# New cost figures and a shared port in the planner that orders a hybrid encoder's instructions

## The chip, the core and the metric

The kernel runs on one core of one Trainium2 chip. A core has five engines, each with an instruction queue of its own that runs in order: TensorE (PE), VectorE (DVE), ScalarE (ACT), GpSimd (POOL) and SyncE (SP), which here issues the DMA transfers. An instruction waits on semaphores for what other engines must have done. The metric is the device time of one execution in microseconds (us).

## What is computed

Two sequences (prompt and sample) of 1024 rows of 1024 channels go through the same two layers and a final norm. Cut to what matters:

```python
def mixer_layer(x, ...):
    hdn = rmsnorm(x, norm_g)
    z = jnp.einsum('bsd,dp->bsp', hdn, w_in)          # 1024 -> 12 blocks of 256
    (a_v, a_g, b_q, b_k, b_v, b_g, c_u, c_g, d_q, d_k, d_v, d_g) = jnp.split(z, N_BLOCKS, axis=-1)
    y_a = pool_mixer(a_v, pool_w, pool_scale) * jax.nn.silu(a_g)
    y_b = dilated_attention(rope(heads(b_q)), rope(heads(b_k)), heads(b_v)) * jax.nn.silu(b_g)
    y_c = s5_mixer(c_u, a_re, a_im, log_dt, b_re, b_im, c_re, c_im, ssm_d, glu_w, glu_b) * jax.nn.silu(c_g)
    y_d = neighbourhood_attention(heads(d_q), heads(d_k), heads(d_v), na_rpb) * jax.nn.silu(d_g)
    y = jnp.concatenate([y_a, y_b, y_c, y_d], axis=-1)
    return x + jnp.einsum('bsm,md->bsd', y, w_out)
```

The S5 mixer is a complex diagonal scan over the 1024 steps, in both directions, whose coefficients depend on the layer's weights alone. Weights and activations are fp32.

## The kernel before

The channels lie on the partitions. A large product (`project`, `output`) is made from an fp32 weight `raw` that is split into a rounded part `whi` (ACT) and a remainder `wlo` (POOL), and from activations split in the same way (`xh` and `xl`, for the output `yh` and `yl`); PE then runs three products of 512 columns for each 128x128 block, into PSUM banks.

The program is recorded, planned and then emitted. `Recorder.record` notes each of 17,631 operations with what it reads and writes, under a thread of work. The threads run over four iterations (both sequences in layer 0, then both in layer 1). One iteration `i` has `na_i` (neighbourhood attention), `dil_i` (dilated attention with the rotary products), `ssm_i` and `sout_i` (the scan, then its gelu and gate), `pool_i`, `out6723_i` and `out_i` (the output product), and `x_{i+1}` loads and splits the next iteration's input. `setup0` and `setup1` build a layer's scan tables: on DVE in the arrays `arena`, `work`, `turns`, `W` and `R`, then by POOL's products `E<-turns`, `u<-turns`, `E<-E,u` (24 instructions a layer). These are stored to DRAM as `Rd` and loaded back as `R`, which the first step of `ssm` multiplies with. `setup0` is recorded ahead of `na_0` and `setup1` in iteration 1; both go with a low rank and are "patient".

The first step of the scan goes by four quads. For one quad PE writes two banks, DVE makes `X<-bank,R` and two partner products, adds them, runs four scans in `X`, and POOL multiplies the result back (`H0`, in the trace `zk<-X,R` and the like); DVE adds into `H`, and PE's next products (`cy`, in the banks `rb` and `ss`) read `H`. The result goes to DRAM (`yd`) and comes back as `cy`.

`Recorder.order` is a greedy list scheduler. It keeps a clock, and for each engine a heap of the operations that are ready at that clock. The free engine takes the ready one with the lowest rank. An operation is ready a latency after each of its inputs has ended: `LAT` by pair of engines, and 150 ns (`SLACK`) more for a patient thread. How long it keeps its engine is `Recorder.cost`. A DMA costs SP 640 ns, and lands by a model of bandwidth. `Recorder.emit` then writes each engine's instructions in the planned order, so every instruction of the trace has that one line, L461, and groups are told apart by tiles. A tile name in the trace is that of the first tile in its slot: `vz` and `kt` are PSUM banks, `zk`, `zq`, `zg`, `zs` and `wto` are one kind of scratch tile in SBUF whatever is in them. In the changed program the line is L476 and the scratch tiles are called `zq`, `zr`, `th`, `fold` and `wto`. The figures of `LAT` and `cost` only decide the order; nothing in the program waits by them.

Of the kernel before, what the change touches and what calls it, by code (L numbers as in the profile page):

```python
# [11 lines left out]
F32R = mybir.dt.float32r  # L12
# [3 lines left out]
PSUM = bass.MemoryType.PSUM  # L16
# [131 lines left out]


class Op:  # L150
    __slots__ = ("eng", "method", "args", "kw", "reads", "writes", "idx", "prio", "thread", "cost", "deps", "outs", "n", "ready", "end", "tiles", "pos", "start", "s", "e", "ev")


class Thread:
# [4 lines left out]
class Engine:  # L159
# [3 lines left out]
    def __getattr__(self, method):  # L163
# [2 lines left out]
        return f  # L166


LAT = {("PE", "DVE"): 196, ("PE", "ACT"): 197, ("DVE", "ACT"): 128, ("ACT", "DVE"): 142, ("DVE", "POOL"): 155, ("POOL", "DVE"): 74,
       ("ACT", "PE"): 664, ("DVE", "PE"): 640, ("POOL", "PE"): 640, ("ACT", "POOL"): 180, ("POOL", "ACT"): 75, ("DVE", "DVE"): 127, ("ACT", "ACT"): 64, ("POOL", "POOL"): 64,  # L170
       ("SP", "PE"): 500, ("PE", "PE"): 0, ("SP", "SP"): 0, ("SP", "DVE"): 0, ("SP", "ACT"): 0, ("SP", "POOL"): 0}
# [5 lines left out]
class Recorder:  # L177
# [26 lines left out]
        self.threads.append(self.thread)  # L204

    def cost(self, op):
        out = op.writes[0]
        n = 1
        for _, c in out.dims[1:]:
            n *= c  # L210
        spaces = [v.tile.space for v in op.reads] + [out.tile.space]
        ps = "PSUM" in spaces
        if op.eng == "PE":
            if op.method == "transpose":
                return 107 * n / 128
            f32r = op.reads[0].dtype == F32R
            return n / 2.4 + 1 if f32r and n >= 256 else max(n, 128) / 0.6 + 1
        if op.eng == "DVE":
            m = op.method
            if m == "reciprocal":  # L220
                return 68 + 6.5 * n / 0.96
            if not ps and m in ("tensor_copy", "tensor_scalar", "tensor_scalar_mul", "memset"):
                return 66 + n * 0.525
            return 68 + n * 1.042 + (8 if m == "tensor_tensor_reduce" else 0) + (61 if isinstance(op.kw.get("scalar"), View) else 0)
        if op.eng == "ACT":
            return (52 if ps else 93) + n * 0.833 + (93 if "accum_out" in op.kw else 0) + (94 if len(op.reads) > 1 else 0)
        if op.eng == "POOL":
            if op.method == "memset":
                return 40 + n * 0.5
            spread = any(s == 0 and c > 1 for v in op.reads for s, c in v.dims[1:])  # L230
            return 148 + n * (1.67 if spread else 2.1)
        return 640

    def record(self, eng, method, args, kw):
        op = Op()
# [68 lines left out]
    def order(self):  # L304
# [14 lines left out]
        dma = 0.0  # L319
        done, result, now = 0, [], 0.0  # L320
        active = list(self.threads)

# [40 lines left out]
        while done < len(self.ops):  # L363
            progress = False
            for e in engines:
                if busy[e] > now:
                    continue
                q, r = later[e], now_ready[e]
                while q and q[0][0] <= now:
                    _, _, op = heapq.heappop(q)  # L370
                    heapq.heappush(r, (op.prio, op.idx, op))
                aside, pick, full = [], None, {}
                while r:
                    x = heapq.heappop(r)
                    if room(x[2], full):
                        pick = x[2]
                        break
                    aside.append(x)
                for x in aside:
                    heapq.heappush(r, x)  # L380
                if pick is None:
                    continue
                op, progress = pick, True
                for t in op.tiles:
                    if t.group and t.slot is None:
                        fs = free[t.group]
                        best = min((f for f in fs if f[0] <= now), key=lambda f: (-f[0], f[1]))
                        fs.remove(best)
                        t.slot = best[1]
                        t.thread.future[t.group][t.users[0].pos :] -= 1  # L390
                        t.thread.most.pop(t.group, None)
                op.start = now
                op.end = now + op.cost
                busy[e] = op.end
                if e == "SP":
                    v = op.writes[0]
                    size = 4
                    for _, n in v.dims:
                        size *= n
                    dma = max(dma, now + 1100) + size / 360.0  # L400
                    op.end = dma + 900
                result.append(op)
                done += 1
                th = op.thread
                op.n = -1
                if th.frontier == op.pos:
                    th.most = {}
                while th.frontier < len(th.ops) and th.ops[th.frontier].n == -1:
                    th.frontier += 1
                if th.frontier == len(th.ops):  # L410
# [67 lines left out]
SSMP, SB, GLU, POOLR, SPLIT, H0Z = (0, 1), "t", 0, 1, 'gpsimd', 1  # L478
# [1329 lines left out]
```

## Time and profile before

| what | us |
|---|---|
| median of three runs (2187.92 to 2194.0) | 2192.05 |
| the profiled execution | 2193.71 |
| its span in the trace | 2191.9 |
| PE busy | 1981.1 |
| DVE busy | 1678.4 |
| ACT busy | 1095.2 |
| POOL busy | 780.5 |

The profile is of one execution. Busy time is the sum of an engine's instruction times, overlaps counted once. Windows of the trace give the same by stretch, the list of waits tells for whom an engine waited, the timeline shows single instructions with start, duration, and in brackets the idle time before them, and the chain goes back from the last instruction to what released each step. TensorE's granted clock is 0.959 of full speed over the run.

### The profile page before, as it was taken

The numbers are of one execution on the slowest core, as the hardware profiler recorded it, in microseconds if no ns is written. First come the engines' busy times: TensorE is split into PE (matmuls) and PEld (weight loads), VectorE is DVE, ScalarE is ACT, GpSimd is POOL, SyncE is SP. The second block draws the span as 40 slices with busy tenths as digits, with TensorE's granted clock in tenths as the row PEclk, the third lists the DMA queues.
The fourth block names the chain that finished last, engine by engine and source line by source line (L and its number), as shares of the span: only waits on it lengthen the run. The fifth ranks groups of instructions, "written<-read, shape, count | busy, mean of one in ns | idle before, by whom it ended". The sixth has DMA issues, their size and how long they took to land.

```text
span 2191.9 us, 32719 instructions
## 1 busy us (share of the span) xinstructions
PE 1981.1 (90%) x10724; PEld 1670.6 (76%) x10724; DVE 1678.4 (77%) x3432; ACT 1095.2 (50%) x2486; POOL 780.5 (36%) x593
## 2 busy tenths in 40 slices
PE   7898899879999999888998999987899999997898
PEld 7677777757888887666786888776679888786677
DVE  7999789996156678899798667889944766899845
ACT  4467575134156678124124668811532766861224
POOL 3214642336221323436226242334544223323334
PEclk8999999999999999989999999998999999998999
DMA  4354524527644323625675533353477434245164
GB/s 138 107 161 126 165 68 125 165 78 238 205 135 134 107 89 94 196 79 174 214 204 154 154 98 101 87 187 95 152 259 253 152 118 131 78 132 163 52 209 156
DMA packets 284986, 313.95 MB, mean 143 GB/s; under 512 B 46736, under 2 KB 192656, under 8 KB 284816
## 3 DMA queue, kind: packets, MB, share of 16 engines
q1 hardware_dynamic: 284816, 311.86, 46.0%
q8 instruction: 85, 1.39, 0.3%
q14 instruction: 85, 0.70, 0.1%
HBM read 235.32 MB, written 78.54 MB: 143 GB/s over the span
## 4 chain that ended last, share of the span: by engine, by line
PE 47%; DVE 28%; issue 9%; DMA 9%; ACT 3%; POOL 3%; SPq 1%; POOLq 0%; DVEq 0%; ACTq 0%
PE vz L461 32%; DVE X L461 7%; PE kt L461 6%; PE no L461 3%; PE rb L461 3%; DMA nv<-vd 3%; PE ss L461 3%; DVE H L461 2%; POOL wlo L461 2%; DVE arena L461 2%; DVE gate L461 2%; DVE zk L461 2%; SPq L461 1%; DVE W L461 1%; DVE kl L461 1%
## 5 line engine op out<-in xcount | busy, mean ns | idle before, releaser
L461 POOL TENSOR_TENSOR wlo<-raw,whi 128x512 fp32r<-128x512 f32 x248 | 369.3, 1490 | 1042.5 <-ACT whi L461 911.3
L461 PE MATMUL vz<-xh,whi 128*128 128x512 f32 x1316 | 529.6, 403 | 4.6 <-DVE gate L461 1.5
L461 PE MATMUL vz<-xh,wlo 128*128 128x512 f32 x1316 | 530.7, 403 | 0.0
L461 PE MATMUL vz<-xl,whi 128*128 128x512 f32 x1316 | 527.9, 401 | 0.3 <-DVE xl L461 0.3
L461 ACT ACTIVATE whi<-raw 128x512 fp32r<-128x512 f32 x248 | 155.7, 628 | 330.8 <-DMA raw<-in_w_out 127.3
L461 PEld LDWEIGHTS vz<-xh,whi 128*128 128x128 f32 x1316 | 250.8, 191 | 49.4 <-DVE gate L461 3.3
L461 PEld LDWEIGHTS vz<-xh,wlo 128*128 128x128 f32 x1316 | 251.1, 191 | 42.4 <-issue 1.4
L461 PEld LDWEIGHTS vz<-xl,whi 128*128 128x128 f32 x1316 | 250.4, 190 | 42.6 <-issue 1.4
L461 PE MATMUL vz<-whi,xh 128*128 128x256 f32 x464 | 135.2, 292 | 12.1 <-ACT xh L461 8.0
L461 ACT ACTIVATE p<-p,st 128x256 f32<-128x256 f32 x256 | 128.1, 502 | 16.7 <-DVE st L461 15.5
L461 PE MATMUL vz<-wlo,xh 128*128 128x256 f32 x464 | 134.9, 292 | 0.3 <-POOL wlo L461 0.2
L461 PE MATMUL vz<-whi,xl 128*128 128x256 f32 x464 | 134.9, 291 | 0.1
L461 DVE TENSOR_TENSOR p<-vz,p 128x512 f32<-128x512 f32 x74 | 50.9, 688 | 88.8 <-PE vz L461 65.6
L461 PE MATMUL vz<-yh,whi 128*128 128x512 f32 x260 | 105.0, 404 | 6.9 <-DVE gate L461 5.9
L461 PE MATMUL vz<-yh,wlo 128*128 128x512 f32 x260 | 104.3, 401 | 0.0
L461 PE MATMUL vz<-yl,whi 128*128 128x512 f32 x260 | 103.8, 399 | 0.0
L461 PEld LDWEIGHTS vz<-whi,xh 128*128 128x128 f32 x464 | 92.0, 199 | 13.6 <-ACT xh L461 8.0
L461 ACT ACTIVATE p<-p,nmx 128x384 f32<-128x384 f32 x128 | 78.4, 613 | 33.1 <-DVE nmx L461 32.4
L461 DVE TENSOR_TENSOR D<-ss,D 128x256 fp32r<-128x256 f32 (+2 forms) x196 | 86.7, 463 | 9.8 <-ACT D L461 8.2
L461 PEld LDWEIGHTS vz<-wlo,xh 128*128 128x128 f32 x464 | 91.9, 198 | 1.3 <-POOL wlo L461 0.7
L461 PEld LDWEIGHTS vz<-whi,xl 128*128 128x128 f32 x464 | 92.2, 199 | 0.9 <-DVE xl L461 0.3
L461 PE MATMUL no<-D,bv 128*128 128x256 f32 x512 | 86.4, 291 | 2.6 <-DVE D L461 1.5
(502 smaller groups left out, 4844.6 us busy)
## 6 DMA issues: line engine op xcount, KB each, us to landing
raw<-in_w_in SPq DMA_DIRECT2D x192, 256.0 KB
x<-p SPq DMA_DIRECT2D x112, 256.0 KB
p<-x SPq DMA_DIRECT2D x88, 256.0 KB
nbias<-in_na_bias SPq DMA_DIRECT2D x48, 384.0 KB
nv<-vd SPq DMA_DIRECT2D x256, 64.0 KB
raw<-in_w_out SPq DMA_DIRECT2D x128, 128.0 KB
vd<-vt SPq DMA_DIRECT2D x16, 512.0 KB
vb<-vt SPq DMA_DIRECT2D x16, 512.0 KB
```

The lines of the kernel that those rows point to most:

```text
L461: getattr(engines[op.eng], op.method)(*[real(a) for a in op.args], **{k: real(v) for k, v in op.kw.items()})
```

## The change

Only the planner's numbers change. The same 17,631 operations are recorded; their order and their slots differ.

- `LAT`: 640 to 664 ns from a vector engine to PE become 55, and 60 (`MARGIN`) for another engine, and 140 (`LOAD`) where the tile is PE's weights. From an engine to itself the latency becomes 0 (DVE had 127, ACT and POOL 64).
- `cost`: for DVE 145 + 1.055 n ns in place of 68 + 1.042 n for n elements of a row, for ACT 180 or 200 in place of 52 or 93 as the constant, for POOL 190 in place of 148, for PE 13.5 in place of 1, and for an issue on SP 60 in place of 640.
- A port: a DVE operation with two wide inputs in SBUF, and a POOL operation with one, is planned to end its cost after the later of the clock and the port's release; POOL's keep the port for 0.7 of their cost.

```diff
-LAT = {("PE", "DVE"): 196, ("PE", "ACT"): 197, ("DVE", "ACT"): 128, ("ACT", "DVE"): 142, ("DVE", "POOL"): 155, ("POOL", "DVE"): 74,
...
+LAT = {("ACT", "DVE"): 33, ("ACT", "PE"): 55, ("ACT", "POOL"): 78, ("DVE", "ACT"): 34, ("DVE", "PE"): 55, ("DVE", "POOL"): 79, ("PE", "ACT"): 215, ("PE", "DVE"): 215,
...
+LOAD, MARGIN = 140, 60
+
+HOLD = 0.7
 SLACK = 150
...
     def cost(self, op):
...
+        wide = [v for v in op.reads if v.tile.space == "SB" and any(c > 1 for _, c in v.dims[1:])]
+        op.port = len(wide) >= 2 if op.eng == "DVE" else op.eng == "POOL" and len(wide) >= 1
...
-            return n / 2.4 + 1 if f32r and n >= 256 else max(n, 128) / 0.6 + 1
+            return n / 2.4 + 13.5 if op.reads[0].dtype == F32R and n >= 256 else max(n, 128) / 0.6 + 9
...
-            return 68 + n * 1.042 + (8 if m == "tensor_tensor_reduce" else 0) + (61 if isinstance(op.kw.get("scalar"), View) else 0)
+            return 145 + n * (1.83 if apart else 1.055) + (85 if m == "tensor_tensor_reduce" else 0) + (60 if isinstance(op.kw.get("scalar"), View) else 0)
         if op.eng == "ACT":
-            return (52 if ps else 93) + n * 0.833 + (93 if "accum_out" in op.kw else 0) + (94 if len(op.reads) > 1 else 0)
+            return (180 if ps else 200) + n * 0.833 + (187 if "accum_out" in op.kw else 0) + (88 if len(op.reads) > 1 else 0)
         if op.eng == "POOL":
...
-            return 148 + n * (1.67 if spread else 2.1)
-        return 640
+            return 190 + n * (1.75 if spread else 2.15)
+        return 60
...
                 op.start = now
-                op.end = now + op.cost
+                op.end = (max(now, port) if op.port else now) + op.cost
+                if op.port:
+                    port = op.end - (1 - HOLD) * op.cost * (e == "POOL")
                 busy[e] = op.end
...
                 for o, raw in op.outs:
-                    lat = LAT.get((e, o.eng), 130)
+                    lat = LAT.get((e, o.eng), 60)
+                    if o.eng != e and e != "SP":
+                        lat += MARGIN
+                    if o.eng == "PE" and o.args[1].tile in op.tiles:
+                        lat += LOAD
                     if o.eng != e and o.thread.patient:
                         lat += SLACK
                     when = op.end + lat if raw else now
```

Three places in the two orders follow. The first is DVE's queue early in iteration 0. `arena`, `work`, `W` and `R` belong to `setup0`; `zq` and `kl` belong to `na_0`, where `kl` is the remainder of its keys, which PE's scores wait for. Before:

```order
158 L461 MEMSET arena_353 128x256
159 L461 TENSOR_TENSOR work_773<-work_773,arena_353 128x256
160 L461 TENSOR_TENSOR W_947<-work_773 128x512
161 L461 SCALAR_TENSOR_TENSOR zq_831<-vz_289,rstd_668 128x512
162 L461 TENSOR_TENSOR R_955<-work_773 128x512
163 L461 TENSOR_TENSOR W_947<-work_773 128x512
164 L461 TENSOR_TENSOR kl_739<-zq_831,K_737 64x512
165 L461 TENSOR_TENSOR W_947<-W_947,R_955 128x512
166 L461 TENSOR_TENSOR kl_740<-zq_831,K_738 64x512
167 L461 TENSOR_TENSOR R_955<-work_773 128x512
168 L461 COPY arena_353<-work_773 64x4x16 x2
169 L461 TENSOR_TENSOR W_947<-W_947,R_955 128x512
```

After, at the same keys:

```order
84 L476 SCALAR_TENSOR_TENSOR zq_750<-vz_296,rstd_670 128x512
85 L476 RECIPROCAL arena_276<-arena_276 128x16
86 L476 TENSOR_SCALAR arena_276<-arena_276 128x16
87 L476 TENSOR_TENSOR arena_276<-arena_276 128x16 x3
88 L476 TENSOR_TENSOR kl_684<-zq_750,K_682 64x512
89 L476 TENSOR_TENSOR arena_276<-arena_276 128x16 x4
90 L476 TENSOR_TENSOR kl_685<-zq_750,K_683 64x512
91 L476 TENSOR_TENSOR arena_276<-arena_276 128x16 x4
92 L476 COPY r_50_898<-arena_276 64x4x2 x2
93 L476 SCALAR_TENSOR_TENSOR zq_750<-vz_316,rstd_670 128x512
94 L476 COPY r_50_898<-arena_276 64x4x2 x2
95 L476 COPY arena_276<-arena_276 128x16 x2
```

The large products of `setup0` stood between the keys of `na_0`; in the new order only its small operations stand there, and they come in runs in which each reads what the one before it wrote.

The second place is POOL's queue, with the products `E` of `setup0`. `turns` is what DVE made for them, `zk`, `zq`, `zg` and `th` hold `u` or rotary values, `wlo` is a weight's remainder. Before, in the middle of `dil_0`:

```order
60 L461 TENSOR_TENSOR E_2189<-E_2189,zk_1005 128x512
61 L461 TENSOR_TENSOR E_2421<-turns_897 128x512
62 L461 TENSOR_TENSOR zk_1005<-turns_897 128x512
63 L461 TENSOR_TENSOR E_2421<-turns_897 128x512
64 L461 TENSOR_TENSOR wlo_262<-raw_248,whi_258 128x512
65 L461 TENSOR_TENSOR E_2421<-E_2421,zk_1005 128x512
66 L461 TENSOR_TENSOR wlo_382<-raw_246,whi_264 128x512
67 L461 TENSOR_TENSOR zk_1005<-turns_897 128x512
68 L461 TENSOR_TENSOR E_2529<-turns_897 128x512
69 L461 TENSOR_TENSOR E_2421<-E_2421,zk_1005 128x512
70 L461 TENSOR_TENSOR zg_1732<-turns_897 128x512
```

After, right ahead of the scan of `ssm_0` (its first POOL product on `X`, `zq_1071<-X_4257`, is row 121, and the last `E` is row 118):

```order
83 L476 TENSOR_TENSOR E_3872<-turns_2971 128x512
84 L476 TENSOR_TENSOR wlo_288<-raw_248,whi_282 128x512
85 L476 TENSOR_TENSOR E_3872<-turns_2971 128x512
86 L476 TENSOR_TENSOR E_3903<-turns_2971 128x512 x2
87 L476 TENSOR_TENSOR E_3929<-turns_2971 128x512
88 L476 TENSOR_TENSOR wlo_366<-raw_248,whi_352 128x512
89 L476 MEMSET zr_1787 128x64
90 L476 TENSOR_TENSOR zq_750<-turns_2971 128x512
91 L476 TENSOR_TENSOR E_3872<-E_3872,zq_750 128x512
92 L476 TENSOR_TENSOR wlo_286<-raw_246,whi_284 128x512
93 L476 TENSOR_TENSOR zq_750<-turns_2971 128x512
94 L476 TENSOR_TENSOR E_3872<-E_3872,zq_750 128x512
```

The 24 products moved from `dil_0` to the last place ahead of `ssm_0`'s first product on this queue; they stand in 36 rows (83 to 118) after and in 35 rows (46 to 80) before.

The third place is POOL's queue in iteration 2, with the products `E` of `setup1`. `kl_9991` and `kl_9992` are cleared for the keys of `na_2`, `cos` and `sin` are the rotary tables of `dil_2`. Before:

```order
295 L461 TENSOR_TENSOR wlo_382<-raw_246,whi_370 128x512
296 L461 TENSOR_TENSOR wlo_270<-raw_246,whi_258 128x512
297 L461 TENSOR_TENSOR E_10195<-turns_9466 128x512
298 L461 MEMSET kl_9991 64x1024
299 L461 TENSOR_TENSOR zs_2283<-turns_9466 128x512
300 L461 MEMSET kl_9992 64x1024
301 L461 TENSOR_TENSOR E_10195<-E_10195,zs_2283 128x512
302 L461 TENSOR_TENSOR wlo_262<-raw_248,whi_264 128x512
303 L461 TENSOR_TENSOR E_10195<-turns_9466 128x512
```

After:

```order
320 L476 MEMSET kl_11009 64x1024
321 L476 MEMSET kl_11010 64x1024
322 L476 TENSOR_TENSOR fold_1350<-fold_1350,cos_10904 128x512
323 L476 TENSOR_TENSOR wlo_288<-raw_246,whi_284 128x512
324 L476 TENSOR_TENSOR E_11437<-turns_9852 128x512
325 L476 TENSOR_TENSOR th_1338<-turns_9852 128x512
326 L476 TENSOR_TENSOR wlo_286<-raw_248,whi_352 128x512
327 L476 TENSOR_TENSOR E_11437<-E_11437,th_1338 128x512
328 L476 TENSOR_TENSOR E_11437<-turns_9852 128x512
```

Before, they stood between the two clearings of `na_2`'s keys; in the new order they stand among `dil_2`'s instructions, behind its first rotary products.

## Rows read from the trace of the kernel before

**Rows 1.** The page: busy time and share by engine, then the chain by engine.

```profile
PE 1981.1 (90%) x10724; PEld 1670.6 (76%) x10724; DVE 1678.4 (77%) x3432; ACT 1095.2 (50%) x2486; POOL 780.5 (36%) x593
...
PE 47%; DVE 28%; issue 9%; DMA 9%; ACT 3%; POOL 3%; SPq 1%; POOLq 0%; DVEq 0%; ACTq 0%
```

**Rows 2.** Windows by iteration: stretch, length; busy of PE, PEld, DVE, ACT, POOL; PEclk, DMA, GB/s.

```profile
0.00:588.50 588.50, 516.89 (x2738) 431.91 (x2739) 481.11 (x1017) 286.29 (x639) 219.92 (x168) 0.95 0.47 144
588.50:1115.00 526.50, 484.28 (x2597) 408.31 (x2596) 397.10 (x867) 263.87 (x604) 171.82 (x128) 0.97 0.45 138
1115.00:1660.40 545.40, 493.98 (x2674) 414.73 (x2673) 419.35 (x796) 275.35 (x623) 217.14 (x165) 0.96 0.48 148
1660.40:2191.90 531.50, 485.99 (x2722) 415.68 (x2720) 380.86 (x753) 269.70 (x621) 171.63 (x134) 0.96 0.45 142
```

**Rows 3.** Windows within iteration 0: setup0's stretch, the E products, ssm_0 to sout_0.

```profile
34.00:201.00 167.00, 151.85 (x809) 123.28 (x808) 150.81 (x494) 89.08 (x223) 32.08 (x25) 0.95 0.46 130
201.00:272.00 71.00, 60.09 (x401) 54.77 (x402) 56.53 (x106) 43.45 (x107) 49.37 (x37) 0.93 0.47 140
...
440.00:544.00 104.00, 88.60 (x372) 68.93 (x371) 86.02 (x109) 47.05 (x71) 49.68 (x33) 0.93 0.49 158
```

**Rows 4.** Window, instructions that touch arena alone: busy of PE, PEld, DVE.

```profile
34.00:201.00 167.00, 6.28 (x64) 3.05 (x64) 48.51 (x220) 0.95 0.46 130
```

**Rows 5.** Timeline of POOL, iteration 0, first and last product of E: start, us, instruction.

```profile
200.83 1.07 POOL L461 TENSOR_TENSOR E<-turns 128x512 f32<-128x512 f32 x1 [0.81 <-DVE turns L461]
...
256.32 1.29 POOL L461 TENSOR_TENSOR E<-E,zk 128x512 f32<-128x512 f32 x1
```

**Rows 6.** Timeline of SP: the load of the table R that ssm_0 begins with.

```profile
354.64 0.60 SPq L461 DMA_DIRECT2D R<-Rd  x1
```

**Rows 7.** The chain in iteration 0: start, us, what; a round through DRAM.

```profile
457.09 4.34 DMA cy<-yd
```

**Rows 8.** Timeline in iteration 2: keys of na_2, the E run, the score product.

```profile
1170.17 8.98 DVE L461 TENSOR_TENSOR kl<-zg,K 64x512 fp32r<-64x512 f32 x2 [0.70 <-ACT K L461]
...
1171.81 1.28 POOL L461 TENSOR_TENSOR E<-E,zs 128x512 f32<-128x512 f32 x1
...
1177.35 1.25 POOL L461 TENSOR_TENSOR E<-E,zs 128x512 f32<-128x512 f32 x1
...
1181.03 0.68 DVE L461 TENSOR_TENSOR kl<-zg,K 64x512 fp32r<-64x512 f32 x1 [0.69 <-ACT K L461]
...
1181.71 0.69 PE L461 MATMUL vz<-K,Q 128*128 128x384 f32 x1 [8.41 <-ACT K L461]
```

**Rows 9.** Waits of PE over the span: total us, times, longest us.

```profile
PE rb L461 <- DVE H L461: 33.7, 6, 5.9
...
PE vz L461 <- ACT K L461: 15.2, 3, 8.4
...
PE ss L461 <- DVE H L461: 12.0, 2, 6.2
...
PE vz L461 <- DVE gate L461: 7.4, 7, 2.3
...
PE vz L461 <- DVE zg L461: 6.6, 6, 3.4
PE vz L461 <- DVE pu L461: 6.1, 7, 1.1
```

**Rows 10.** Timeline of DVE in ssm_1: two independent steps, then a scan behind its input.

```profile
947.58 0.68 DVE L461 TENSOR_TENSOR wto<-vz,R 128x512 f32<-128x512 f32 x1
948.18 0.68 DVE L461 SCALAR_TENSOR_TENSOR gate<-zq,zg 128x512 f32<-128x512 f32 x1
...
951.69 0.67 DVE L461 TENSOR_TENSOR X<-X,zq 128x512 f32<-128x512 f32 x1
952.40 1.22 DVE L461 TENSOR_TENSOR_SCAN X<-zs,X 64x512 f32<-64x512 f32 x1
```

**Rows 11.** The page's costliest groups: the weight remainder on POOL; the count, then busy, mean ns.

```profile
L461 POOL TENSOR_TENSOR wlo<-raw,whi 128x512 fp32r<-128x512 f32 x248 | 369.3, 1490 | 1042.5 <-ACT whi L461 911.3
```

More of the change, by code (lines that the diff above doesn't have):

```diff
@@ L150 @@
 class Op:
-    __slots__ = ("eng", "method", "args", "kw", "reads", "writes", "idx", "prio", "thread", "cost", "deps", "outs", "n", "ready", "end", "tiles", "pos", "start", "s", "e", "ev")
+    __slots__ = ("eng", "method", "args", "kw", "reads", "writes", "idx", "prio", "thread", "cost", "deps", "outs", "n", "ready", "end", "tiles", "pos", "start", "s", "e", "ev", "port")
 class Thread:
@@ L166, in __getattr__ @@
         return f
-LAT = {("PE", "DVE"): 196, ("PE", "ACT"): 197, ("DVE", "ACT"): 128, ("ACT", "DVE"): 142, ("DVE", "POOL"): 155, ("POOL", "DVE"): 74,
-       ("ACT", "PE"): 664, ("DVE", "PE"): 640, ("POOL", "PE"): 640, ("ACT", "POOL"): 180, ("POOL", "ACT"): 75, ("DVE", "DVE"): 127, ("ACT", "ACT"): 64, ("POOL", "POOL"): 64,
-       ("SP", "PE"): 500, ("PE", "PE"): 0, ("SP", "SP"): 0, ("SP", "DVE"): 0, ("SP", "ACT"): 0, ("SP", "POOL"): 0}
+LAT = {("ACT", "DVE"): 33, ("ACT", "PE"): 55, ("ACT", "POOL"): 78, ("DVE", "ACT"): 34, ("DVE", "PE"): 55, ("DVE", "POOL"): 79, ("PE", "ACT"): 215, ("PE", "DVE"): 215,
+       ("POOL", "ACT"): 33, ("POOL", "DVE"): 34, ("POOL", "PE"): 55, ("SP", "PE"): 100, ("PE", "PE"): 0, ("DVE", "DVE"): 0, ("ACT", "ACT"): 0, ("POOL", "POOL"): 0}
+LOAD, MARGIN = 140, 60
+HOLD = 0.7
 SLACK = 150
@@ L210, in cost @@
             n *= c
-        spaces = [v.tile.space for v in op.reads] + [out.tile.space]
-        ps = "PSUM" in spaces
+        ps = "PSUM" in [v.tile.space for v in op.reads] + [out.tile.space]
+        wide = [v for v in op.reads if v.tile.space == "SB" and any(c > 1 for _, c in v.dims[1:])]
+        op.port = len(wide) >= 2 if op.eng == "DVE" else op.eng == "POOL" and len(wide) >= 1
+        m = op.method
         if op.eng == "PE":
-            if op.method == "transpose":
-                return 107 * n / 128
-            f32r = op.reads[0].dtype == F32R
-            return n / 2.4 + 1 if f32r and n >= 256 else max(n, 128) / 0.6 + 1
+            if m == "transpose":
+                return 108 * n / 128
+            return n / 2.4 + 13.5 if op.reads[0].dtype == F32R and n >= 256 else max(n, 128) / 0.6 + 9
@@ L218, in cost @@
         if op.eng == "DVE":
-            m = op.method
             if m == "reciprocal":
-                return 68 + 6.5 * n / 0.96
+                return 145 + 6.1 * n
             if not ps and m in ("tensor_copy", "tensor_scalar", "tensor_scalar_mul", "memset"):
-                return 66 + n * 0.525
-            return 68 + n * 1.042 + (8 if m == "tensor_tensor_reduce" else 0) + (61 if isinstance(op.kw.get("scalar"), View) else 0)
+                return (66 if m == "memset" else 145) + n * 0.55
@@ L225, in cost @@
+            if m == "tensor_tensor_scan":
+                return 145 + 2.1 * n
+            step = [s for s, c in out.dims[1:] if c > 1]
+            apart = n >= 256 and step and abs(step[-1]) >= 4
+            return 145 + n * (1.83 if apart else 1.055) + (85 if m == "tensor_tensor_reduce" else 0) + (60 if isinstance(op.kw.get("scalar"), View) else 0)
         if op.eng == "ACT":
-            return (52 if ps else 93) + n * 0.833 + (93 if "accum_out" in op.kw else 0) + (94 if len(op.reads) > 1 else 0)
+            return (180 if ps else 200) + n * 0.833 + (187 if "accum_out" in op.kw else 0) + (88 if len(op.reads) > 1 else 0)
@@ L227, in cost @@
         if op.eng == "POOL":
-            if op.method == "memset":
-                return 40 + n * 0.5
+            if m == "memset":
+                return 100 + n * 0.8
             spread = any(s == 0 and c > 1 for v in op.reads for s, c in v.dims[1:])
-            return 148 + n * (1.67 if spread else 2.1)
-        return 640
+            return 190 + n * (1.75 if spread else 2.15)
+        return 60
     def record(self, eng, method, args, kw):
@@ L318, in order @@
                 heapq.heappush(later[op.eng], (0.0, op.idx, op))
-        dma = 0.0
+        dma = port = 0.0
         done, result, now = 0, [], 0.0
```

## Prediction

> **What bounds the kernel now.** I read the page first: PE is busy 1981.1 us of a span of 2191.9, DVE 1678.4, and the chain that ended last runs 47% through PE and 28% through DVE [rows 1]. So there are some 211 us in which PE stands, and DVE is the second bound. Then the windows by iteration [rows 2]: PE's idle time (length less busy) is 71.6, 42.2, 51.4 and 45.5 us. Iterations 0 and 2 hold more: `setup0` runs in the one, and the products of `setup1` in the first tenth of the other (1167 to 1179 us [rows 8]). Iterations 1 and 3 have about 44 us of it without that. The reader should see that an order that hid both setups wholly could win at most 27.7 + 7.5 = 35 us by that, and that a part of the 27.7 is the start, which no order removes.
>
> Then the stretches of iteration 0 [rows 3]. From 34 to 201 us DVE is busy 150.8 of 167 and PE stands 15.2; from 201 to 272, while POOL makes the products E, PE stands 10.9; from 440 to 544, in the scan and its gate, 15.4. The waits of PE [rows 9] name the rest: the largest, 33.7 and 12.0 us in eight waits of up to 6.2, are for `H`, the end of a quad of the scan. There DVE is the bound, and one order for another only moves where PE stands.
>
> **What the new numbers get wrong.** A DVE row of 512 lasts 0.68 us, but the next independent one starts 0.60 us after its start (947.58, 948.18), while a scan that reads the row before it starts after 0.71 (951.69, 952.40) [rows 10]. The old planner charged 68 + 1.042 x 512 = 601 ns and 127 more for a dependent one, 728: both close. The new one charges 145 + 1.055 x 512 = 685 ns for either. For it a dependent successor is free, where the chip makes DVE lose 0.71 - 0.60 = 0.11 us. The orders show what follows: neighbours on DVE of which the second reads the first were 179 and are 443. The 264 more cost 264 x 0.11 = 29 us of DVE, if all were on the path. The Trainium skill's page "Perfetto Trace Analysis", section "Optimizing Scalar/DVE Operations", speaks against the change in the same way: an access overhead of about 60 ns per DVE instruction, of which the profile's duration shows twice, since the half for the write acknowledgement overlaps with the next instruction. By its 60 ns the pairs would cost, as an estimate, 16 us in place of 29.
>
> **Part by part.** The sum is made against the profiled execution, 2193.7 us (span 2191.9 and 1.8 around it), which lies 1.7 above the median of the runs.
>
> *Setup0 spread out.* Its DVE work stood in a block at 34 to 201 us, with 48.5 us in the instructions that touch `arena` alone [rows 4], and in the large products between the keys of `na_0`. In the new order the small ones stand between them and the large ones later, to the end of `dil_0`. PE's 15.2 us there go, I take it. The 10.9 of the next stretch stay, since the work arrives there instead and DVE waits for PE's scores anyway. -15; bounds 0 and -26 (both stretches).
>
> *The tables of ssm_0 come late.* In the old order the first E starts at 200.8 and the last at 256.3 [rows 5], and the load of R is issued at 354.6 [rows 6]: 97 us of cover. In the new order the block ends three rows ahead of `ssm_0`'s first product on POOL. The cover is gone, so what was free now counts: a store and a load through DRAM. The only hop of this kind with a price on the path is the 4.34 us of `cy<-yd` [rows 7]; two of them are about 9. What shortens it is that DVE and PE have `pool_0` and the splits of `x_1` put ahead of `ssm_0`, as cover for the products themselves. If that covers the hops too, 0. If POOL meets DVE at the port, each of the 24 products takes longer, at the mean of `wlo`, 1.49, in place of 1.29, or 5 us in all [rows 5, 11], or twice that in a thick place: 20. I take +9, bounds 0 and +20.
>
> *Setup1 moved behind na_2's keys.* At 1170.17 two `kl` instructions take 8.98 us, where one takes 0.68 eleven us later. POOL runs six instructions back to back meanwhile (from the E at 1171.81 to that at 1177.35), five of them setup1's, and PE then waits 8.41 us for its keys [rows 8]. In the new order the block stands among `dil_2`'s instructions. -8.4; bounds 0, where another `kl` meets it, and -8.4. The Trainium skill's page "SBUF — State Buffer", section "Terms", says that the port which DVE and GpSimd share is an exclusive lock, held for one instruction by whoever has it. The row does not agree, as far as it goes: the wait is some 7.6 us long, six POOL instructions and not one. By the Trainium skill's page a `kl` would lose no more than an instruction, about 1.3 us, the 8.4 would have another cause and the move would win about nothing; the sum would be 2184.
>
> *Small waits and the pairs, all iterations.* PE's latencies fall from 640 to 115 or 255 ns, and in the new order of PE more large products stand ahead of what has to wait. The waits for `gate`, `zg` and `pu`, 7.4 + 6.6 + 6.1 = 20.1 us [rows 9], have this form. I take half, -10; bounds 0 and -20. Against it stand the pairs. Where PE is the bound DVE's idle time hides them (in iteration 3 DVE is busy 380.9 of 531.5 [rows 2]). Where DVE is the bound, in `ssm`, `sout` and `pool`, the orders count 72 more, 72 x 0.11 = +8; bounds 0 and +29 for all. Together -2.
>
> *Left alone.* Issues of SP are planned at 60 ns, where the load of R holds it 0.60 us [rows 6]. This I cost at nothing: 1657 issues of some 0.5 us are 830 us of a queue with 2192. Bursts in it lie beside PE's work; where the cover is gone, it is a part of the +9. The waits for `H`, 45.7 us, stay as they are: POOL's products and DVE's adds of one quad are the same.
>
> Sum: 2193.7 - 15 + 9 - 8.4 - 2 = 2177.3 in the terms of the profiled run, so 2176 against a median of 2192.05. By iteration that is -6 in iteration 0, -8.4 in 2, and nearly nothing in 1 and 3.
>
> **The rivals.**
>
> *Nothing gained (2190).* The scan, the gate and `pool` are bound by DVE, and the block of setup0 is as long wherever it stands. PE's idle time only moves: from the keys of `na_0` to the first `H` of `ssm_0`. Then of the four terms only a few us of setup1 are left. For it speaks that DVE has 481.1 us in iteration 0, against 380.9 in iteration 3, and none of it is removed; against it, that PE's work in the same iteration is 516.9, still more [rows 2].
>
> *Slower by the port (2215).* POOL's E run now stands where DVE has its two-input instructions thickest, the shifted sums of `pool_0` and the scan of `ssm_0`. If DVE loses there what `kl` lost, 7.6 us for six POOL instructions [rows 8], the 36 rows of the block cost it 6 x 7.6 = 46 us, less the 8 to 9 in which the hops would have been waited for anyway: 2177 + 38 = 2215. It decides from 16 us on, or two such meetings, since then no gain is left. For it: the planner thinks the port is free again after 0.7 of POOL's cost, so it sees no queue there. Against: in 201 to 272 the same block ran beside a DVE that was busy 56.5 of 71 us, without such a loss [rows 3]. The lock of the Trainium skill's page "SBUF — State Buffer", section "Terms", would rule it out, since a loser waits there for one instruction only.
>
> *Slower by thin margins (2210).* PE was planned to start 640 ns after DVE, now 115 to 255. DVE and POOL run later than planned at the port, and PE's queue is in order, so each late row stops the large products behind it. If the waits for `gate`, `zg`, `pu` and K, 20.1 + 15.2 = 35 us [rows 9], double in place of being halved, the sum is 2176 + 35 = 2211.
>
> *More gained (2148).* All of PE's idle time in 34 to 272 goes, the hops are hidden, all small waits go: 2193.7 - 26 - 8.4 - 20 + 8 = 2147.
>
> **How the numbers follow.** My forecast, 2160 to 2187, has 0.42; more gained 0.13; nothing gained 0.20; the port 0.15; thin margins 0.10. Runs of this kernel differ by 0.3%, 6.6 us, which is what a measurement can tell from no change. Faster by more is 0.42 + 0.13 = 0.55, the same 0.20, slower 0.25. The range reaches from 2150, near the larger gain, to 2210, to leave out a tenth on each side: the half of the port's case and part of the others.
>
> **What would show it.** In the changed profile: iteration 0 ends some 6 us earlier, and DVE is busy less in its first 200 us; the load of R is issued only just ahead of the first `X` of `ssm_0`; no `kl` of several us at na_2's keys, and no wait of 8 us for K; waits for `H` still above 40 us. I would be wrong if the E block of iteration 0 carries DVE rows of several us (the port), if PE's waits for `gate`, `zg`, `nmx` and K grow (margins), or if iterations 1 and 3, which have no setup in the way, change by more than 5 us: then the order of the large products does more than I can read from the rows.

## Result and profile after

The changed kernel takes 2314.18 us (median of four runs, 2312.97 to 2317.11), against 2193.03 before: a ratio of 1.0559 (95% interval 1.0538 to 1.0579). The forecast was 2176, with 2150 to 2210 as its range. It is 121 us slower.

The page of the changed kernel, busy times and then TensorE's granted clock in 40 slices:

```profile
PE 2005.0 (87%) x10724; PEld 1685.7 (73%) x10724; DVE 1721.7 (74%) x3432; ACT 1113.0 (48%) x2486; POOL 777.3 (34%) x593
...
PEclk9999999769999999987999999998899999999799
```

PE stands 2311.2 - 2005.0 = 306 us, where it stood 211 [rows 1]: 95 of the loss are idle time. Another 24 us are in PE's busy time, 2005.0 against 1981.1 for the same instructions. The granted clock accounts for nearly all of these: weighted with the clock granted at each moment, the two busy times are 1923.4 and 1919.1 us.

Windows of the changed kernel by iteration, cut where each `out` ends, with the columns of [rows 2]:

```profile
0.00:619.00 619.00, 516.54 (x2739) 434.47 (x2739) 496.56 (x1018) 289.74 (x639) 217.02 (x168) 0.92 0.45 137
619.00:1174.00 555.00, 490.33 (x2577) 412.67 (x2577) 402.04 (x841) 267.41 (x601) 173.57 (x127) 0.94 0.41 129
1174.00:1746.00 572.00, 501.79 (x2687) 416.79 (x2687) 430.77 (x822) 281.96 (x626) 212.16 (x165) 0.96 0.48 143
1746.00:2311.20 565.20, 496.33 (x2725) 421.77 (x2723) 392.31 (x753) 273.86 (x621) 174.59 (x134) 0.94 0.42 133
```

The iterations take 30.5, 28.5, 26.6 and 33.7 us more. Iterations 1 and 3 lose as much as those with a setup. So the setup's place, on which the forecast spent most of its words, can't be the main reason for the loss.

The waits of PE in the changed kernel (total us, times, longest), against [rows 9]:

```profile
PE no L476 <- DMA nv<-vd: 47.0, 35, 2.6
PE ss L476 <- DVE H L476: 25.7, 4, 10.5
PE rb L476 <- DVE H L476: 21.8, 5, 19.1
...
PE vz L476 <- ACT K L476: 12.4, 5, 3.8
PE no L476 <- DMA bv<-vb: 10.9, 4, 3.8
...
PE vz L476 <- DVE gate L476: 9.4, 7, 3.1
```

Before, the row of `nv` was:

```profile
PE no L461 <- DMA nv<-vd: 13.2, 17, 1.6
```

`nv<-vd` has become the largest; `bv<-vb`, which before was not among the waits of PE, is new at 10.9. The waits for `H` are 25.7 + 21.8 = 47.5 against 45.7.

Where PE's idle time lies by thread was added up from the trace, as the gap between each PE instruction and the end of the last before it, put to the thread of the later one. "All" is over all threads; it is less than span minus busy by the start and the end. "Busy" is PE's busy time, and "at full clock" the same, each moment weighted with the granted clock. The kernels below the first two are explained in the next section.

| kernel | na_0 to na_3 | dil | ssm | sout, pool | all | busy | at full clock |
|---|---|---|---|---|---|---|---|
| before | 32.6 | 31.2 | 79.9 | 22.0 | 196.1 | 1981.1 | 1919.1 |
| after | 67.4 | 49.2 | 106.6 | 40.3 | 290.7 | 2005.0 | 1923.4 |
| SP undone (u1) | 14.3 | 23.4 | 95.5 | 65.2 | 239.8 | 1978.3 | 1918.6 |
| SP alone (s1) | 85.6 | 48.0 | 48.1 | 30.0 | 246.6 | 2012.5 | 1927.3 |
| durations alone (s4) | 24.7 | 32.5 | 162.3 | 35.5 | 292.8 | 2007.9 | 1917.9 |
| durations undone (u3) | 65.7 | 40.5 | 34.3 | 41.2 | 232.7 | 2007.0 | 1926.5 |
| port undone (u4) | 74.8 | 78.6 | 93.3 | 40.1 | 317.0 | 2020.6 | 1920.2 |
| port alone (s3) | 27.3 | 24.4 | 24.6 | 49.4 | 168.5 | 1986.2 | 1925.5 |
| SP and durations undone (c1) | 23.1 | 18.4 | 35.8 | 52.0 | 141.7 | 1960.4 | 1922.0 |

In these nine the last column differs by less than 10 us: where PE's busy time differs, it is nearly all by the clock.

### The profile page after: what moved, and what is told of

Read it like the earlier page. It is cut to its first block, busy times and chain, and to the rows that moved or that the text cites. A ratio compares the mean times of both kernels' runs of the same rounds, so it can differ in the third digit from the quotient of the medians.

```text
span 2311.2 us, 32758 instructions
## 1 busy us (share of the span) xinstructions
PE 2005.0 (87%) x10724; PEld 1685.7 (73%) x10724; DVE 1721.7 (74%) x3432; ACT 1113.0 (48%) x2486; POOL 777.3 (34%) x593
## 5 line engine op out<-in xcount | busy, mean ns | idle before, releaser
L476 POOL TENSOR_TENSOR wlo<-raw,whi 128x512 fp32r<-128x512 f32 x248 | 354.3, 1430 | 1213.4 <-ACT whi L476 1113.7
L476 PE MATMUL vz<-whi,xh 128*128 128x256 f32 x512 | 148.3, 293 | 19.1 <-ACT xh L476 10.0
L476 PE MATMUL vz<-whi,xl 128*128 128x256 f32 x512 | 148.8, 291 | 1.0 <-DVE xl L476 0.9
L476 PE MATMUL vz<-wlo,xh 128*128 128x256 f32 x512 | 147.9, 290 | 0.1
L476 PE MATMUL vz<-yh,whi 128*128 128x512 f32 x324 | 130.2, 403 | 12.5 <-DVE gate L476 5.7
L476 PE MATMUL vz<-yl,whi 128*128 128x512 f32 x324 | 129.1, 399 | 1.6 <-DVE yl L476 1.5
L476 PE MATMUL vz<-yh,wlo 128*128 128x512 f32 x324 | 128.4, 397 | 0.0
L476 DVE TENSOR_TENSOR p<-vz,p 128x512 f32<-128x512 f32 x91 | 62.2, 688 | 86.8 <-PE vz L476 48.3
L476 PE MATMUL no<-D,nv 128*128 128x256 f32 x384 | 71.9, 297 | 53.3 <-DMA nv<-vd 47.0
L476 PEld LDWEIGHTS no<-D,nv 128*128 128x128 f32 x384 | 56.0, 192 | 73.5 <-issue 29.9
L476 PE MATMUL no<-D,bv 128*128 128x256 f32 x512 | 89.3, 295 | 21.2 <-DMA bv<-vb 10.9
```

The costliest lines, as they stand in the source:

```text
L476: getattr(engines[op.eng], op.method)(*[real(a) for a in op.args], **{k: real(v) for k, v in op.kw.items()})
```

## The experiments

The change has four parts: SP's numbers, the latencies between PE, DVE, ACT and POOL, the durations (with the latency of an engine to itself), and the port rule. SP's numbers are the issue, 640 to 60 ns, and SP's latencies, 500 to 100 ns to PE and 0 to 60 to the others; the list of the change ahead of the prediction has only the first. (For `nv`, which is PE's weights, the changed planner adds `LOAD`'s 140 to the 100; s1 does not.) Each part was undone alone in the changed planner (u), and put alone into the planner before (s). Everything else is as in the one or the other; the program and its operations are the same.

| kernel | us | ratio to before (95% interval) |
|---|---|---|
| u1 SP undone | 2240.67 | 1.0231 (1.0159 to 1.0304) |
| u2 latencies undone | 2302.89 | 1.0516 (1.0475 to 1.0556) |
| u3 durations undone | 2256.17 | 1.0302 (1.0261 to 1.0344) |
| u4 port undone | 2354.63 | 1.0752 (1.0711 to 1.0793) |
| s1 SP alone | 2274.68 | 1.0391 (1.0360 to 1.0422) |
| s2 latencies alone | 2215.34 | 1.0120 (1.0091 to 1.0149) |
| s3 port alone | 2172.31 | 0.9915 (0.9893 to 0.9938) |
| s4 durations alone | 2317.39 | 1.0582 (1.0544 to 1.0619) |
| u5 SP's issue alone undone | 2278.09 | 1.0407 (1.0363 to 1.0450) |
| c1 SP and durations undone | 2119.35 | 0.9682 (0.9653 to 0.9710) |
| c2 c1, own latencies 0 | 2180.82 | 0.9949 (0.9924 to 0.9974) |
| c3 SP undone, DVE and ACT by their step | 2241.87 | 1.0237 (1.0172 to 1.0301) |
| d1 c1 with PE's new duration | 2208.83 | 1.0063 (1.0040 to 1.0086) |
| d2 c3 with PE's old duration | 2192.18 | 0.9996 (0.9981 to 1.0010) |
| d3 before with PE's new duration | 2225.74 | 1.0144 (1.0114 to 1.0173) |
| d4 after with PE's old duration | 2437.04 | 1.1107 (1.1074 to 1.1139) |
| e1 after, setup0 ranked first | 2342.36 | 1.0711 (1.0662 to 1.0760) |
| e2 c1 with an issue of 450 ns | 2130.63 | 0.9743 (0.9697 to 0.9788) |

### SP's numbers

u1:

```diff
-("SP", "PE"): 100
+("SP", "PE"): 500, ("SP", "SP"): 0, ("SP", "DVE"): 0, ("SP", "ACT"): 0, ("SP", "POOL"): 0
...
-        return 60
+        return 640
```

> The changed planner, with only SP's part undone: an issue costs 640 ns again in the plan, and SP's latency to PE is 500. Theory A (in na_1 to na_3 PE waits for nv<-vd because the plan thinks four loads are issued in 240 ns, where they take about 0.5 us each): the waits of PE for nv<-vd fall from 47.0 us to below 20, bv<-vb from 10.9 to below 5, and the time from 2314 to about 2275. Theory B (the loss is the planner's DVE cost and latency, whose order also sets when nv's slot comes free): nv's waits stay above 40, time 2314 +- 10.

s1 is the same edit the other way, in the planner before:

> The planner before with only SP's numbers changed (issue 60, latency to PE 100, to the others 60). If SP's numbers are a loss of their own: waits for nv rise from 13.2 to about 45 and PE's idle time in na_1 to na_3 from 21 to about 55, time 2192 + 40 = 2230. If they hurt only with the other new numbers: 2185 to 2200, nv's waits below 20.

u5 undoes the 60 alone and leaves the 100:

> The changed planner with one number undone: an issue on SP costs 640 ns in the plan, its latency to PE stays at 100. If the issue cost is what made PE wait for nv<-vd (four loads planned in 240 ns): nv's waits fall from 47 to below 20 as with both numbers undone (10.4), time 2240 to 2270. If it is the latency of 500 that covered the landing: waits stay above 35, time about 2300.

The waits of PE for `nv<-vd`, first in u1, then in s1:

```profile
PE no L494 <- DMA nv<-vd: 10.4, 15, 1.7
```

```profile
PE no L492 <- DMA nv<-vd: 73.1, 49, 3.0
```

Undone, 47.0 us of waits become 10.4 and 73 us of time come back; alone, 13.2 become 73.1 and 85 us are lost. Theory A, a loss of SP's own, holds in both directions; theory B is out as the reason for these waits. The same split runs through all twenty kernels: with both of SP's new numbers PE waits 36 to 73 us for `nv`, otherwise 8 to 20. With the issue alone undone the waits fall to 16.0, so most of them belong to the issue; but only 36 us come back, since PE's idle time in `ssm` grows to 128.7 there (106.6 in the changed kernel). So the time does not follow these waits alone.

How the plan's figure gets into PE's queue is seen in one unit of `na_1`. The timeline of the changed kernel (start, us, instruction, idle before it):

```profile
680.37 1.69 SPq L476 DMA_DIRECT2D nv<-vd  x3
...
685.68 0.87 PE L476 MATMUL no<-D,nv 128*128 128x256 f32 x5 [1.75 <-DMA nv<-vd]
```

The timeline of the kernel before, at the same place:

```profile
701.63 1.68 SPq L461 DMA_DIRECT2D nv<-vd  x3
...
708.40 0.86 PE L461 MATMUL no<-D,nv 128*128 128x256 f32 x5 [0.23 <-DMA nv<-vd]
```

In both, SP issues three of the unit's four loads of `nv` one by one, half a microsecond each, right behind PE's products on the old content, and PE's next five products wait for them. Before, these start 6.77 us after the first of the issues and waited 0.23 of that; after, they start 5.31 us after it and waited 1.75. So PE was ready for them 6.5 us after the first issue before, and 3.6 us after: the transfer is no slower, the product stands nearer to it. Counted in the order: from the PE instruction that last reads a part of `nv` to the first that reads its new content there are 33 PE instructions before (median of the 60 loads of `na_1`), 25 after, 25 in s1, 32 in u1. Between the two stand 17, 12, 12 and 17 of the large products of 512 columns. With loads that cost next to nothing in the plan, the planner brought the products forward and spent fewer of the large ones on the gap.

### The durations

u3 gives back the old `cost` and the 127 and 64 ns from an engine to itself:

```diff
-            return 145 + n * (1.83 if apart else 1.055) + ...
+            return 68 + n * 1.042 + ...
-("DVE", "DVE"): 0, ("ACT", "ACT"): 0, ("POOL", "POOL"): 0
+("DVE", "DVE"): 127, ("ACT", "ACT"): 64, ("POOL", "POOL"): 64
...
```

> The changed planner with the durations of PE, DVE, ACT and POOL as before, and with 127 and 64 ns from an engine to itself; dependent neighbours on DVE fall from 473 to 209 in the order. Theory B (durations and pairs): most of the 121 us comes back, time 2190 to 2220. Theory A with late tables: nv's waits stay near 47 us; the tables E end earlier in this order, so ssm_0's share, 30 us, comes back; time 2270 to 2290.

s4 puts the new ones alone into the planner before:

> The planner before with only the durations changed (and 0 ns from an engine to itself). Dependent neighbours on DVE rise from 236 to 517 in the order. If the durations are a loss of their own: 2192 + 58 = 2250, with 27 to 31 us more in the pairs and PE's idle time in ssm grown. If they hurt only with the others: 2185 to 2205.

58 us come back undone, between the two expectations, and 128 are lost alone, the largest single loss. It lies elsewhere than SP's: in s4 PE stands 24.7 us in `na` and 162.3 in `ssm` (the table). One such place is in the timeline of s4, at the last quad of `ssm_1`:

```profile
1020.04 0.69 DVE L494 TENSOR_TENSOR zg<-kt,R 128x512 f32<-128x512 f32 x1 [1.65 <-DMA yd<-zg]
...
1021.49 3.36 DVE L494 TENSOR_TENSOR_SCAN X<-fold,X 64x512 f32<-64x512 f32 x2
...
1029.05 0.68 DVE L494 TENSOR_TENSOR H<-X,zq 64x508 f32<-64x508 f32 x1
1029.65 0.68 DVE L494 TENSOR_TENSOR H<-X,zg 64x508 f32<-64x508 f32 x1
...
1029.84 1.35 PE L494 MATMUL rb<-H,Cm 128*128 128x128 f32 x4 [12.57 <-issue]
```

DVE's first step of this quad waits for a DMA that still reads its tile; then come the scans; PE stands 12.57 us, put down to no engine, and starts at 1029.84, 0.11 us after the end of the `H` begun at 1029.05. By that it was `H` that it waited for, and the order had put no large product in this gap. Beside the scan of `ssm_1` (from the first `X` to the last `H`) lie 238 planned PE instructions in s4 in 101.7 us, 267 in 85.3 before, and 311 in 84.5 in c1: in s4 PE runs dry where the order put too few products beside a stretch in which DVE is the bound. In the changed kernel this fits `ssm_0` alone, whose idle time rose from 20.4 to 49.9 us; that of the other three together went from 59.6 to 56.7.

c1 undoes SP's numbers and the durations, and leaves the latencies and the port:

> The changed planner with SP's numbers and the durations undone; the latencies between engines and the port rule stay. If the two losses add (73 and 58 us of the 122): 2314 - 131 = 2183, within 0.5% of before. If they overlap, or latencies and port carry a loss of their own: 2210 to 2240.

The page of c1:

```profile
PE 1960.4 (93%) x10724; PEld 1648.9 (78%) x10724; DVE 1645.5 (78%) x3432; ACT 1102.9 (52%) x2486; POOL 792.4 (37%) x593
...
PEclk9999999999999999998999999999899999999999
```

c1 is 3.2% faster than the kernel before, and beats both kernels and both expectations. That is more than the two losses together would explain: 2314 - 73 - 58 = 2183, and it takes 2119. With the durations already undone SP's numbers are worth 137 us (u3 to c1), and with SP's undone the durations are worth 121 (u1 to c1). PE stands 157 us (2117.7 - 1960.4), 36 of it in `ssm` by the table, where it was 80.

Which of the durations loses? Own latencies of 0, put into c1:

```diff
-("DVE", "DVE"): 127, ("ACT", "ACT"): 64, ("POOL", "POOL"): 64
+("DVE", "DVE"): 0, ("ACT", "ACT"): 0, ("POOL", "POOL"): 0
```

> As the kernel with SP's numbers and the durations undone (2119), but with 0 ns from DVE, ACT and POOL to themselves. Dependent neighbours on DVE rise from 160 to 496 in the order, nothing else is planned otherwise. Theory pairs: 336 x 0.11 = 37 us of DVE, of which a third to all counts: 2131 to 2156. Theory charge (the harm of the durations is that DVE and ACT are planned 77 to 150 ns too long per row): 2119 +- 8.

The page of c2:

```profile
PE 1983.5 (91%) x10724; PEld 1662.2 (76%) x10724; DVE 1705.5 (78%) x3432; ACT 1104.8 (51%) x2486; POOL 782.7 (36%) x593
```

The zeros cost 61 us, more than either expectation, and DVE's busy time grows from 1645.5 to 1705.5. The order has 336 more dependent neighbours on DVE, 160 to 496 (here every order that the program fixes counts; the prediction's 179 and 443 are those in which the second reads what the first wrote). At 0.11 us each they account for 37 us; where the rest arises was not traced. So the zero from an engine to itself is a loss of its own on this base, of more than the time of its pairs.

c3 keeps the new figures but charges DVE and ACT by the step:

```diff
-            return 145 + n * (1.83 if apart else 1.055) + (85 if ...
+            return 67 + n * (1.83 if apart else 1.055) + (8 if ...
-            return (180 if ps else 200) + n * 0.833 + (187 if ...
+            return (52 if ps else 93) + n * 0.833 + (93 if ...
-("DVE", "DVE"): 0, ("ACT", "ACT"): 0, ("POOL", "POOL"): 0
+("DVE", "DVE"): 112, ("ACT", "ACT"): 64, ("POOL", "POOL"): 64
```

> SP undone, new latencies, port rule, and the new durations of PE and POOL and of DVE's special rows, but DVE and ACT charged by the step from one row to the next (67 + 1.055 n; ACT 52 or 93) and 112 or 64 ns for a dependent one. With DVE and ACT charged by their full duration and 0 it took 2241. If it is DVE's and ACT's overcharge and the free dependence that hurt: 2105 to 2130, with some 190 dependent neighbours. If PE's or POOL's new figures hurt: 2180 to 2240.

2242, as with the full durations (u1, 2241). So neither the overcharge nor the free dependence is what is left, once PE's, POOL's and the scan's new figures are in. Four kernels then moved PE's figure alone:

```diff
-            return n / 2.4 + 1 ...
+            return n / 2.4 + 13.5 ...
```

> The kernel with SP's numbers and the durations undone (2119), with PE's new duration alone put in (13.5 in place of 1 ns per product, what the trace's step shows). Theory PE's figure (an undercharged PE puts more large products ahead of each wait, and so covers what DVE does late): a loss of 40 to 120, time 2160 to 2240. Theory DVE's scan or POOL's figures: 2119 +- 10.

> The step-based kernel (2242) with PE's duration undone. Theory PE's figure: 2120 to 2140, as the kernel with all durations undone. Theory DVE's scan or POOL's figures: 2220 to 2250.

> The planner before with PE's new duration alone. In its plan 229 PE instructions lie beside the scan of ssm_1, where the plan before had 265. Theory PE's figure: PE's idle time in ssm rises from 80 us over four iterations to about 120, time 2230 to 2260. Otherwise 2185 to 2200.

> The changed kernel with PE's duration alone undone. Theory PE's figure: 2314 - 60 or more, below 2260. Otherwise 2300 to 2330; the waits for nv<-vd stay near 47 us in both.

It costs 89 us put into c1, 32 put into the kernel before, and 50 come back undone in c3; but undone in the changed kernel it costs 123 more, where neither expectation came. So PE's new figure, which is nearer to the trace (products of 512 columns follow one another at some 0.23 us there, and it plans 0.227 in place of 0.214), is a loss on three bases and a help on the fourth.

The theory, that an undercharged PE covers what DVE does late, fits none of the three by its mechanism. By it PE's idle time in `ssm` had to grow with the new figure. It went from 35.8 to 34.1 us (c1 to d1), from 79.9 to 62.4 (before to d3, where about 120 was expected) and from 31.6 to 24.5 (d2 to c3). In d3 all of PE's idle time is as before, 196.9 against 196.1, and the loss is in its busy time, 2012.1 against 1981.1; at full clock that is 1943.4 against 1919.1, so 24 of the 31 us are not the clock's. The same instructions took longer in that order, and why is open. In d1 it is 25 us in the same way, beside 42 of idle time outside `ssm`. d2, expected at 2120 to 2140, took 2192.

### Latencies and port

> The changed planner with only the latencies between PE, DVE, ACT and POOL as before (640 to 664 to PE; margin and load 0). Theory thin margins (PE's queue stops at rows that are planned 115 to 255 ns after their input): the waits of PE for gate, zr, fold, nmx, p, ct and D, some 60 us, halve, time about 2270. Theory A with the late tables of ssm_0: waits for nv stay at about 47 us, the first X of ssm_0 moves with E, time 2290 to 2314.

> The planner before with only the latencies between PE, DVE, ACT and POOL changed (115 or 255 to PE in place of 640). Thin margins: PE waits for gate, zg, nmx and K grow by some 20 to 35 us, time 2210 to 2225. If they are nearer to the chip and no loss: 2180 to 2195, and PE's idle time in ssm, 80 us in four iterations before, does not grow.

> The changed planner with the port rule off (no instruction holds it). In this order the E products of setup0 end early on POOL, well ahead of ssm_0's first X. Late tables: the 30 us of PE's idle time in ssm_0 come back, time about 2275, nv's waits stay near 47. Theory B: no change beyond 10 us, 2305 to 2320.

> The planner before with only the port rule added. The kernel with SP's numbers and the durations undone was 3.2% faster than before, while the latencies alone were 1.2% slower; what is left there is the port rule. If the rule itself is the gain: 2120 to 2150, and DVE's time at the port (instructions longer than the trace shows them alone) falls below the 237 us of before. If it needs the new latencies: 2185 to 2215.

The edits: `LAT` between engines as before with `MARGIN` and `LOAD` at 0 (u2), or new (s2); `op.port = False` (u4), or the rule alone (s3). The latencies lose 26 us alone; the 11 in the changed kernel are not clear of noise, since the intervals of the two ratios overlap. The port rule gains 17 alone, where neither expectation came, and 40 in the changed kernel, where undoing it was expected to win 40 or to change nothing: it is the one part that helps wherever it was tried. Together the two gain 70 (c1), where alone they sum to a loss of 9. So they depend on each other; why was not tested.

### The tables of ssm_0

e1 ranks `setup0` like the other threads in the changed kernel and does not hold it back, so that the tables are early:

```diff
-                    nc.base = LATE
-                    nc.thread.patient = True
+                    nc.base = LATE if name[5:] != "0" else 0
+                    nc.thread.patient = name[5:] != "0"
```

> The changed kernel, but setup0 is ranked like the other threads and not held back, so its E products end about 180 us ahead of the first X of ssm_0 in the order. Theory late tables: PE's idle time in ssm_0 falls from 50 to about 20, at the price of the ping-pong in na_0 (up to +15): time 2285 to 2300. Theory order of the scan itself (as with the port undone): it stays at 40 to 50 us, time 2310 or more. nv's waits stay near 47 in both.

It takes 28 us more than the changed kernel, as the second expectation allows. PE's idle time in `ssm_0` falls from 49.9 to 33.9, between the two, and that in `na_0` rises from 11.3 to 32.8. With the port undone (u4) the last `E` ends at 326.8 us, 44 ahead of the first `X`, and `ssm_0` has 48.8 us still. So late tables are a part of `ssm_0`'s loss at most, and this order, which has them early, pays more elsewhere.

### SP's true issue time

> The fastest kernel (2119) with SP's issue planned at 450 ns, about what the trace shows for one, in place of 640; its latency to PE stays at 500. If only a figure far below the true one harms: 2110 to 2135, nv's waits below 15 us. If 640 was a margin that the loads need (they land 4 us after the issue, where the plan has 2.2): nv's waits rise above 20, time 2140 to 2160.

The waits of PE in e2:

```profile
PE no L492 <- DMA nv<-vd: 17.1, 28, 1.5
```

450 ns in place of 640 in the fastest kernel raises the waits for `nv` from 7.7 to 17.1 us, and the time from 2119 to 2131. The waits are between the two expectations, the time is the first's. The intervals of the two ratios just overlap, so 450 ns costs little if anything, where 60 cost much.

## Why the prediction was wrong, point by point

**The step that failed first is "Left alone".** It cost SP's 60 ns at nothing, since SP's queue is not full over the run, and did not name the latency of 500 that became 100. But the plan's figures do not act on SP's load. They act on how many PE instructions the order leaves between the release of a buffer and its next use, and for `nv` that is 33 before and 25 after. SP's two numbers are worth 73 us undone and 85 alone. No rival had them.

**The durations were priced by the pairs alone.** The term was +8, bounds 0 and +29. The mechanism is there (c2), but for 61 us on that base. As a group the durations are worth 58 to 128 us, most of it in `ssm`, in PE's idle time and not in DVE's rows. The prediction took "the waits for `H` stay as they are" from the fact that DVE's work in a quad is the same; in s4 what changes is how many products the order lays beside it. In the changed kernel the waits that the profile puts to `H` did stay, 47.5 us against 45.7, but one of them grew to 19.1 us.

**Setup0 spread out (-15).** Windows of the changed kernel in iteration 0, against [rows 3]:

```profile
34.00:201.00 167.00, 158.17 (x899) 136.31 (x898) 139.11 (x414) 101.58 (x247) 43.90 (x34) 0.98 0.38 115
201.00:272.00 71.00, 56.01 (x351) 47.14 (x350) 63.96 (x157) 41.82 (x111) 4.48 (x3) 0.93 0.46 128
445.00:545.00 100.00, 58.40 (x278) 50.64 (x279) 86.47 (x96) 21.29 (x33) 40.54 (x32) 0.71 0.47 150
```

PE's idle time from 34 to 201 us falls from 15.2 to 8.8, and from 201 to 272 rises from 10.9 to 15.0. The direction was right, and the size was 2 us for both together.

**The tables late (+9).** They came as late as the order said. The timeline of SP, then of DVE, in the changed kernel:

```profile
438.32 0.57 SPq L476 DMA_DIRECT2D R<-Rd  x1
```

```profile
442.20 0.69 DVE L476 TENSOR_TENSOR zr<-kt,R 128x512 f32<-128x512 f32 x1 [2.02 <-DMA R<-Rd]
```

The load of R is issued at 438.3, 3.9 us ahead of the row that waits for it. In the last of the windows above PE stands 41.6 us of 100, against 15.4 in 104 before [rows 3]. +26 for this stretch where the sum had +9; but in e1 early tables alone did not win it back.

**Setup1 moved (-8.4).** It came true: the longest wait for K is 3.8 us, where it was 8.4 [rows 8, 9]. In `na_2` PE stands 19.2 us all the same, 14.4 before, since the waits for `nv` are there too.

**Small waits (-10).** They did not halve: `gate` is 9.4 against 7.4. The new latencies are a loss of 26 us alone and of 11 at most in the changed kernel.

**The rivals.** The port was the wrong way round: its rule gains, and while POOL made the products E no DVE row of 512 took more than 1.8 us. That a loser at the port waits for one instruction only, as the prediction worked out from the lock, has its own [rows 8] against it, 7.6 us beside six instructions; no run here tests it. Thin margins are a small part; its sum, 2176 + 35, still held the -10 for the same waits halved, so it should have been at least 2221. "Nothing gained" was right that PE's idle time moves to the scan, and silent on its growth. Of the signs named for being wrong, the last one came: iterations 1 and 3 changed by more than 5 us, by 28.5 and 33.7.

What stays open: which of the new durations does the harm in the changed kernel, why PE's busy time grew in d1 and d3 by more than the clock, and why the parts do not add. Shown is that SP's numbers and the durations as a group lose on every base that was tried, three each, and that with both undone the other two gain 3.2%.

## What to carry to other kernels

A list scheduler's figures are not a description but a lever: a figure decides how much other work the order leaves between two operations. Here an issue priced at 60 ns took cover away from loads that follow a freed buffer. Change one group of figures at a time, and count in the order what stands between the release of a slot and its next use, on the queue that will wait. A figure nearer to the trace can make the time worse, as PE's did on three bases; measure it before it replaces the old one, and on more than one base, since it helped on the fourth.

## What the runs showed of the hardware

I had not expected that the waits would show in the clock as they do. PE's waits in `ssm_0` of the changed kernel, from the timeline:

```profile
445.54 2.08 PE L476 MATMUL vz<-UM,B 128*128 128x128 f32 x8 [10.28 <-DVE X L476]
...
460.24 1.40 PE L476 MATMUL ss<-H,Cm 128*128 128x128 f32 x4 [10.49 <-DVE H L476]
...
484.20 1.35 PE L476 MATMUL rb<-H,Cm 128*128 128x128 f32 x4 [19.08 <-DVE H L476]
```

and the windows around them (PEclk is the eighth figure, ahead of the DMA share and GB/s):

```profile
450.00:460.20 10.20, 0.00 (x0) 0.00 (x0) 9.08 (x9) 2.07 (x3) 6.62 (x7) 0.50 0.16 51
...
465.00:484.00 19.00, 0.12 (x2) 0.00 (x0) 18.44 (x19) 0.60 (x1) 3.88 (x2) 0.58 0.16 53
484.00:494.00 10.00, 8.16 (x44) 7.38 (x45) 7.61 (x12) 3.39 (x5) 6.24 (x4) 0.78 0.64 189
494.00:504.00 10.00, 4.65 (x22) 4.23 (x20) 8.21 (x9) 0.04 (x1) 4.65 (x5) 0.57 0.77 236
504.00:514.00 10.00, 5.96 (x29) 5.44 (x29) 8.24 (x12) 3.58 (x5) 1.64 (x3) 0.58 0.44 142
514.00:524.00 10.00, 10.00 (x46) 8.18 (x45) 9.90 (x11) 2.83 (x5) 3.87 (x3) 1.00 0.52 172
```

From 450 to 460 and from 465 to 484 us PE did next to nothing, and the granted clock was 0.50 and 0.58: the lower of its two levels (1.2 GHz) for most of it. It was 0.78 in the ten us that followed, with PE busy 8.2. In the next twenty PE was busy about half the time, and the clock was 0.57 and 0.58. It was at the upper level (2.4 GHz) from 514 on. So a part of the products behind a long wait ran at the lower level, and the wait was paid once more in them. Over the run PE was busy at the lower level for 163 us, where it was 124 before: 39 us more at half the rate, which makes 20 of the 24 us of busy time.

SP alone (s1) shows it too: the mean clock over the run is 0.956, hardly below the 0.959 of before, but while PE is busy it is 0.958 against 0.969, and PE's busy time is 31 us longer. The mean clock of a run holds its idle time as well, and so tells little of what the clock cost.
